# Sample tokens of a hybrid decoder layer: the threshold search spread over the projection blocks, the attention placed beside the first feed-forward half

## The chip, the core and the metric

The kernel runs on one core of a Trainium2 chip. The metric is the device time of one execution in microseconds. Before the change it is 2087.43 us, the median of 3 runs (2083.59 to 2090.55).

## What is computed

One layer for 1024 prompt tokens and 8 sample tokens (one new token each, with 4096 cached positions). One input projection feeds two head groups: sparse softmax attention, whose positions an indexer picks, and an RWKV-7 recurrence. Their outputs go through one output projection and a SwiGLU feed-forward. What matters here is the sample tokens' attention:

```python
def sample_attention(q, k_new, v_new, qi, ki_new, wi, cache_k, cache_v, cache_ik, page_table):
    ...
    score = indexer_scores(qi, ki_all, wi)           # 4096 cached positions and the new one
    ...
    _, idx = lax.top_k(score, n_sel)                 # 256 of them
    ...
    return attend_selected(q, pick(cache_k, k_new), pick(cache_v, v_new), valid)

def decoder_layer(x, c, attn_fn, prev_row, s0, lp):
    ...
    att = attn_fn(q, k, v, qi, ki, wi).reshape(B, T, ATT_W)
    rw, s_fin, last_row = rwkv7_mix(pr, prev_row, s0, lp)
    x = x + gate1 * (jnp.concatenate([att, rw], axis=-1) @ lp['w_out'])
    h2 = rms_norm(x, lp['norm2_g']) * (1 + scale2) + shift2
    ffn = (jax.nn.silu(h2 @ lp['w_ffn_gate']) * (h2 @ lp['w_ffn_up'])) @ lp['w_ffn_down']
    return x + gate2 * ffn, (k, v, ki, s_fin, last_row)
```

## The kernel before

Every large product is done as three matmuls on float32r halves (`mm_fm`, line 270 of the profile): each weight tile is loaded raw by SyncE's queue (SP, line 1625), rounded by ScalarE (`fh`, line 1629), and the rest is taken by VectorE or GpSimd (`fl`, line 1630). A projection block is 128 output columns: 8 contraction tiles x 3 products x 3 column groups = 72 matmuls.

In the program's order the stages are: modulation and norm; indexer scores of the prompt; then `qkv` with 12 projection blocks and `rw_project` with 14; the prompt's threshold search (`idx_select`, 26 halvings on VectorE and ScalarE); prompt attention in 4 head pairs of the first 512 queries (`att_pair`), 32 chunks of the modulation weights (`mod_chunk`, line 183; its row is copied by line 186 and transposed by line 189), the RWKV recurrence in 16 units (`rw_run`), attention of the second 512 queries; the output projection of the first half (`out_part`, line 1555); the feed-forward of the first half (`ffn`, gate and up in line 270, down in line 1666) in 10 pairs of 128 columns; the sample tokens' recurrent step (`smp_rwkv`) and `shift_out`; the output projection of the second half with the sample tokens; the last pair of the first half; the feed-forward of the second half.

This is the order of the trace only. The framework plans the instructions of each engine ahead of the run: on each engine an instruction that is ready in the plan goes first if it was traced first, and later work fills what is left. On the chip every engine and every DMA queue then runs its list strictly in order. `issue_after(ins)` is an edge without a wait: instructions traced in its block stand behind `ins` on the engine that they share.

The sample tokens' work up to their attention is a generator, `sample()`: `smp_scores` (16 groups of cached indexer keys, one `yield` each), `smp_select` and `smp_att`. `side(n)` pulls n steps. `SQ` gives the steps after each block of `qkv`, `SP_` those before each block of `rw_project`; all are 3, 78 in all, and 53 are wanted.

`smp_select` finds the 256th largest score per sample token. It opens with the largest and smallest score (a transpose, line 774, and a broadcast product, line 780), then runs 13 iterations: VectorE compares 256 scores per partition with 3 thresholds (line 796) and counts (line 797), TensorE sums the counts over the partitions with a matrix of ones (`allsum`, line 742), VectorE moves the lower bound. Each iteration ends in a `yield`, so its sum is traced in the same step as its count. After a last sum come the list of chosen rows (8 one-hot steps, line 869) and its way through DRAM into `kvrow`, the row numbers for the gathers; `seln` says whether the new token is chosen.

`smp_att` gathers for each of the 8 tokens 256 key rows (two indirect DMAs from GpSimd's queue, line 1285), loads the new key's row (line 1288) and the query spread over 128 partitions (line 1297) over SP, mixes the new row in (lines 1289, 1290), multiplies (line 1298) and sums (line 1299) on VectorE; then the softmax (lines 1303 to 1313); then the same gathers for the values and 4 matmul passes a token (line 1323), with lines 1331 and 1335 taking the heads apart. The query has one buffer, the large tiles four. The result goes to `d_mix[4]` (line 1339).

`smp_rwkv` uses a pool of its own, `smp3`, opened when the recurrence's pool `tR` is closed. It writes the other half of `d_mix[4]` (line 1471). The pools of the second half (`h2B`, `wfB`) are opened after `smp3` and the recurrence's constants are closed; `out_part` loads `d_mix` there (line 1524).

Of the kernel before, what the change touches and what calls it, by code (L numbers as in the profile page):

```python
# [7 lines left out]
F32 = mybir.dt.float32  # L8
F32R = mybir.dt.float32r
BF16 = mybir.dt.bfloat16  # L10
I32 = mybir.dt.int32
# [7 lines left out]
NS = 8  # L19
# [3 lines left out]
CW = 344  # L23
# [12 lines left out]
def bc(ap, shape):  # L36
    return ap.to_broadcast(list(shape))
# [29 lines left out]
WA = (2, 2, 2)  # L67
WB = (3, 3, 3)
SPL = 0
SQ = (3, 3, 3, 3, 3, 3, 3, 3, 3, 3, 3, 3)  # L70
SP_ = (3, 3, 3, 3, 3, 3, 3, 3, 3, 3, 3, 3, 3, 3)


class Ring:
# [10 lines left out]
class Kern:  # L85
# [253 lines left out]
    def rw_project(self, h, wp, tp, side):  # L339
        nc = self.nc  # L340
        for n_, j in enumerate([12, 13] + [o + p for p in range(4) for o in (4, 0, 8)]):
            side(SP_[n_])
            w = self.wload(self.I["w_in"][0], ATT_COLS + 128 * j, 128, wp)
            pr = tp.tile([128, NT + 1], F32, name="pr", bufs=2)
            X = tp.tile([128, T], F32, name="X", bufs=2)
            nc.gpsimd.memset(pr[:, 0:1], 0.0)
            for c in range(NC3):
                ps = self.ps.tile([128, 512], F32, name="ps")
                self.mm_fm(ps, CW, w, 0, 128, h, CW * c)
                nc.scalar.activation(pr[:, 1 + CW * c:1 + CW * c + CW], ps[:, :CW], AF.Copy)  # L350
                n = min(CW, T - CW * c)
                nc.scalar.activation(X[:, CW * c:CW * c + n], ps[:, :n], AF.Copy, scale=self.omm[:, j:j + 1])
            nc.vector.scalar_tensor_tensor(X, pr[:, 0:T], self.prm("rw_mu", j), X, op0=OP.mult, op1=OP.add)
            nc.gpsimd.tensor_copy(self.sh[:, j, :], pr[:, T:T + 9])
            nc.sync.dma_start(self.d_x[j], X)
# [383 lines left out]

    def allsum(self, x, n):  # L740
        ps = self.pS.tile([128, 512], F32, name="ps")
        self.nc.tensor.matmul(ps[:, :n], self.ones, x, start=True, stop=True)
        return ps[:, :n]

    def smp_prefix(self, x, rs, out, tp):
# [18 lines left out]
    def smp_select(self, tp, sp, dp):  # L764
        nc = self.nc
        v = sp.tile([128, 10, NS], F32, name="sbis")
        lo, hi, w, mid, cnt, t, new, tmp = (v[:, k, :] for k in range(8))
        s3 = self.ss.rearrange("p (b z) l -> p b (z l)", z=2)
        mm = tp.tile([128, 16], F32, name="mm", bufs=1)
        nc.vector.tensor_reduce(mm[:, 0:8], s3, axis=AX.X, op=OP.max)  # L770
        nc.vector.tensor_reduce(mm[:, 8:16], s3, axis=AX.X, op=OP.min)
        nc.vector.tensor_scalar(mm[:, 8:16], mm[:, 8:16], -1.0, None, op0=OP.mult)
        ps = self.pS.tile([128, 512], F32, name="ps")
        nc.tensor.transpose(ps[:16, :128], mm, self.ident)
        m1 = tp.tile([16, 1], F32, name="m1", bufs=1)
        nc.vector.tensor_reduce(m1, ps[:16, :128], axis=AX.X, op=OP.max)
        m2 = tp.tile([16, 16], F32, name="m2", bufs=1)
        nc.vector.tensor_scalar(m2, self.ident[:16, :16], m1, None, op0=OP.mult)
        ps = self.pS.tile([128, 512], F32, name="ps")
        nc.tensor.matmul(ps[:, :16], self.ones[:16, :], m2, start=True, stop=True)  # L780
        nc.vector.tensor_tensor(hi, ps[:, 0:8], self.snew, op=OP.max)
        nc.vector.scalar_tensor_tensor(lo, ps[:, 8:16], -1.0, self.snew, op0=OP.mult, op1=OP.min)
        self.bis_open(lo, hi, w, t)
# [7 lines left out]
        for k in range(self.NIT // 2):  # L791
            nc.vector.tensor_scalar(wk, w, 0.25 ** (k + 1), None, op0=OP.mult)
            nc.vector.tensor_tensor(md, fr, up(wk), op=OP.mult)
            nc.vector.tensor_tensor(md, md, up(lo), op=OP.add)
            cmp_ = tp.tile([128, 3, NS, 32], F32, name="sa_", bufs=self.SB["sa_"])
            nc.vector.tensor_tensor(cmp_, bc(s3[:, None], [128, 3, NS, 32]), bc(md[:, :, :, None], [128, 3, NS, 32]), op=OP.is_ge)
            nc.vector.tensor_reduce(cn, cmp_, axis=AX.X, op=OP.add)
            nc.vector.tensor_tensor(nw, up(self.snew), md, op=OP.is_ge)
            ps = self.allsum(cn.rearrange("p j b -> p (j b)"), 3 * NS)
            nc.vector.tensor_tensor(cn, ps.rearrange("p (j b) -> p j b", j=3), nw, op=OP.add)  # L800
            nc.vector.scalar_tensor_tensor(cn, cn, TOPK - 0.5, up(wk), op0=OP.is_ge, op1=OP.mult)
            nc.vector.tensor_reduce(t, cn.rearrange("p j b -> p b j"), axis=AX.X, op=OP.add)
            nc.vector.tensor_tensor(lo, lo, t, op=OP.add)
            yield
        self.bis_close(lo, hi, w, t)
        sel = tp.tile([128, 16, 16], F32, name="sc_", bufs=self.SB["sc_"])
        tie = tp.tile([128, 16, 16], F32, name="sc_", bufs=self.SB["sc_"])
# [8 lines left out]
        nc.vector.tensor_tensor(gtn, self.snew, hi, op=OP.is_gt)  # L816
        nc.vector.tensor_tensor(tin, self.snew, lo, op=OP.is_ge)
        nc.vector.tensor_tensor(tin, tin, gtn, op=OP.subtract)
        ps = self.allsum(cnt, NS)
        nc.vector.tensor_tensor(cnt, ps, gtn, op=OP.add)  # L820
        nc.vector.tensor_scalar(t, cnt, -1.0, TOPK + 0.5, op0=OP.mult, op1=OP.add)
# [6 lines left out]
        nc.vector.tensor_tensor(sel, sel, pf, op=OP.add)  # L828
        nc.vector.scalar_tensor_tensor(tmp, tot, 1.0, t, op0=OP.add, op1=OP.is_le)
        nc.vector.tensor_tensor(tmp, tmp, tin, op=OP.mult)  # L830
        self.seln = sp.tile([128, NS], F32, name="seln")
        nc.vector.tensor_tensor(self.seln, gtn, tmp, op=OP.add)

        self.smp_prefix(sel, rs, pf, tp)
# [21 lines left out]
        for z in range(2):  # L856
            c = slice(128 * z, 128 * z + 128)
            ps = self.pS.tile([128, 512], F32, name="ps")
            for k0 in range(0, 32, 8):
# [8 lines left out]
                for k in range(8):  # L868
                    nc.tensor.matmul(ps[0:64, 0:64], oh[:, k].rearrange("p b h -> p (b h)"), ov[:, k].rearrange("p b h -> p (b h)"),
                                     start=(k0 + k == 0), stop=(k0 + k == 31))  # L870
# [4 lines left out]
            nc.vector.tensor_reduce(l1, t4.rearrange("p b l -> p l b"), axis=AX.X, op=OP.add)  # L875
            nc.vector.tensor_copy(li[:, z, :], l1)
            nc.sync.dma_start(d[4 * z:4 * z + 4].rearrange("b (s l) -> (b s) l", l=16), li[:, z, :])
        self.kvrow = sp.tile([128, NS, 2], I32, name="kvrow")
        for z in range(2):
            nc.sync.dma_start(self.kvrow[:, :, z], d[:, 128 * z:128 * z + 128].rearrange("b s -> s b"))  # L880

# [22 lines left out]
    def qkv(self, h, wp, tp, cp2, side):  # L904
        nc, I = self.nc, self.I
# [9 lines left out]
        for j in range(12):  # L915
            n, p = "qkv"[j // 4], j % 4
            w = self.wload(I["w_in"][0], 128 * j, 128, wp)
            f = tp.tile([128, NT], F32, name="F", bufs=2)
            for c in range(NC3):
                ps = self.ps.tile([128, 512], F32, name="ps")  # L920
                self.mm_fm(ps, CW, w, 0, 128, h, CW * c)
                nc.scalar.activation(f[:, CW * c:CW * c + CW], ps[:, :CW], AF.Copy)
            y = tp.tile([128, 9, 128], F32, name="y", bufs=1)
            if n != "v":
# [1 line left out]
            for g in range(3):  # L926
                ps = self.ps.tile([128, 512], F32, name="ps")
# [18 lines left out]
            nc.sync.dma_start(outs[n][1][:, cs], y[:NS, 8, :])  # L946
            side(SQ[j])

# [777 lines left out]
    def build(self):  # L1726
        tc, nc, I, O = self.tc, self.nc, self.I, self.O
        with ExitStack() as ctx:
# [17 lines left out]
            if True:  # L1746
                with ExitStack() as c1:
# [3 lines left out]
                    with (tc.tile_pool(name="mA", bufs=2) as mp, tc.tile_pool(name="h1x", bufs=3) as xp,  # L1751
                          tc.tile_pool(name="h1f", bufs=1) as fp):
                        self.xt = []
                        c = self.craw = mp.tile([9, D], F32, name="c_raw", bufs=1)
# [11 lines left out]
                        h = self.norm_T(hp, mp, xp, fp)  # L1766
# [3 lines left out]
                    smp = cS.enter_context(tc.tile_pool(name="smp", bufs=1, side="right"))  # L1770
# [14 lines left out]
                    def sample():  # L1785
                        yield from self.smp_scores(smp, rp)
                        yield from self.smp_select(smp, rp, dp)
                        yield from self.smp_att(smp)

                    sgen = sample()  # L1790

                    with tc.issue_after(self.lastmm.ins):
# [39 lines left out]
            smp = cr.enter_context(tc.tile_pool(name="smp2", bufs=1, side="right"))  # L1832
# [32 lines left out]
            self.SB = {"sa_": 4, "sc_": 6}  # L1865
            self.pS = Ring(self.psr, self.psr, self.psr, self.psc)
            with tc.tile_pool(name="smp3", bufs=1) as smp:
                self.smp_rwkv(smp, dp)
                self.shift_out(smp)
            ce.close()  # L1870
# [51 lines left out]
```

## Time and profile before

| | us |
|---|---|
| median of 3 runs | 2087.43 |
| lowest, highest | 2083.59, 2090.55 |
| the profiled execution | 2080.43 |
| its span, first to last instruction | 2078.6 |
| TensorE busy | 1946.7 |
| VectorE busy | 1225.0 |
| ScalarE, GpSimd busy | 796.7, 793.4 |

The span is about 2 us shorter than the execution. [...] Overlapping matmuls count as busy once, and a busy TensorE at half clock does half the work. A wait is put down to the engine whose signal came last.

### The profile page before, as it was taken

To read this page: it belongs to the slowest core of one execution; us is meant where nothing else is said; L and a number is where in the kernel's file an instruction comes from. 1 tells how busy PE (TensorE), PEld (TensorE's weight loads), DVE (VectorE), ACT (ScalarE), POOL (GpSimd) and SP (SyncE) were. 2 spreads that over 40 slices of the span, in tenths; PEclk is the share of its full clock that TensorE was granted. 3 is DMA by queue.
4 is the path that set the end of the run, shared out by engine and by line. 5 is a ranking of instruction groups with operands and counts; after the bars stand their busy time and mean duration, and the time that the engine had idled before them with its cause. 6 is when DMAs were issued, how large, how long until landed. Compare 5 with 4: busy or idle time off the path is not lost.

```text
span 2078.6 us, 38421 instructions
## 1 busy us (share of the span) xinstructions
PE 1946.7 (94%) x14794; PEld 1677.5 (81%) x14794; DVE 1225.0 (59%) x2980; ACT 796.7 (38%) x1590; POOL 793.4 (38%) x1381
## 2 busy tenths in 40 slices
PE   5999999889996998999997979999999999999998
PEld 3878898879993567777766957777888999999998
DVE  6777988997547565667666354557544453121225
ACT  5466667523322343555544332222322332222221
POOL 2411255443454064667555420100411344545452
PEclk8999999989996787999998989999999999999999
DMA  8311233333238574232215322333633324323233
GB/s 262 87 31 31 63 112 97 92 86 107 72 123 261 146 187 114 62 78 76 54 37 157 92 81 84 123 118 113 177 101 104 102 92 142 91 93 92 92 93 113
DMA packets 303204, 220.25 MB, mean 106 GB/s; under 512 B 67151, under 2 KB 281650, under 8 KB 303022
## 3 DMA queue, kind: packets, MB, share of 16 engines
q1 hardware_dynamic: 298140, 200.99, 32.9%
q0 software_dynamic: 4864, 16.78, 2.6%
q8 instruction: 116, 1.90, 0.4%
q14 instruction: 66, 0.54, 0.1%
q10 hardware_dynamic: 18, 0.04, 0.0%
HBM read 187.11 MB, written 30.13 MB: 105 GB/s over the span
## 4 chain that ended last, share of the span: by engine, by line
PE 61%; DMA 7%; DVE 3%; POOL 2%; issue 1%; SPq 1%; ACT 1%; DVEq 0%; ACTq 0%; POOLq 0%
PE ps L270 27%; PE ps L1666 11%; PE ps L1555 3%; PE ps L1264 2%; PE ps L1253 2%; PE ps L1233 1%; PE ps L972 1%; DMA qt<-out_dram 1%; DMA d_t<-arr 1%; PE ps L183 1%; PE ps L388 1%; POOL itmp L1021 1%; PE ps L1052 1%; PE ps L1234 1%; PE ps L1059 1%
## 5 line engine op out<-in xcount | busy, mean ns | idle before, releaser
L1629 ACT ACTIVATE fh<-fr 128x1024 fp32r<-128x1024 f32 (+1 forms) x183 | 190.8, 1055 | 508.6 <-PE ps L270 278.6
L1630 POOL TENSOR_TENSOR fl<-fr,fh 128x1024 fp32r<-128x1024 f32 (+1 forms) x109 | 264.6, 2433 | 312.7 <-ACT fh L1629 310.5
L270 PE MATMUL ps<-h2hi,fh 128*128 128x264 f32 (+2 forms) x1056 | 337.2, 321 | 2.3 <-ACT fh L1629 1.9
L270 PE MATMUL ps<-h2lo,fh 128*128 128x264 f32 (+2 forms) x1056 | 335.8, 319 | 1.0 <-DVE h2lo L1604 1.0
L270 PE MATMUL ps<-h2hi,fl 128*128 128x264 f32 (+2 forms) x1056 | 333.4, 320 | 3.2 <-DVE fl L1630 3.0
L270 PE MATMUL ps<-h1hi,fh 128*128 128x344 f32 (+1 forms) x752 | 250.7, 333 | 1.9 <-ACT rl L556 1.3
L270 PE MATMUL ps<-h1lo,fh 128*128 128x344 f32 (+1 forms) x752 | 247.6, 329 | 0.0
L270 PE MATMUL ps<-h1hi,fl 128*128 128x344 f32 (+1 forms) x752 | 246.9, 328 | 0.0
L270 PEld LDWEIGHTS ps<-h2hi,fh 128*128 128x128 f32 x1056 | 199.0, 189 | 19.2 <-ACT fh L1629 6.0
L270 PEld LDWEIGHTS ps<-h2hi,fl 128*128 128x128 f32 x1056 | 197.7, 188 | 20.4 <-DVE fl L1630 6.9
L270 PEld LDWEIGHTS ps<-h2lo,fh 128*128 128x128 f32 x1056 | 199.0, 188 | 14.6 <-DVE h2lo L1604 1.4
L1021 POOL TENSOR_TENSOR itmp<-la,arr 128x24 f32<-128x24 f32 (+23 forms) x496 | 131.5, 265 | 181.9 <-DMA la<-d_l 146.0
L1655 DVE TENSOR_TENSOR fa<-fa,ps 128x256 f32<-128x256 f32 (+1 forms) x66 | 33.8, 512 | 255.1 <-PE ps L270 255.0
L1666 PE MATMUL ps<-al,fh 128*128 128x512 f32 (+2 forms) x528 | 165.6, 319 | 0.2 <-DVE al L1657 0.2
L1677 DVE TENSOR_TENSOR acc<-acc,ps 128x512 f32<-128x512 f32 (+2 forms) x224 | 107.7, 514 | 88.8 <-PE ps L1666 88.5
L1666 PE MATMUL ps<-ah,fl 128*128 128x512 f32 (+2 forms) x528 | 159.8, 319 | 0.0
L1666 PE MATMUL ps<-ah,fh 128*128 128x512 f32 (+2 forms) x528 | 156.9, 321 | 0.0
L270 PEld LDWEIGHTS ps<-h1hi,fh 128*128 128x128 f32 x752 | 144.2, 192 | 8.2 <-ACT rl L556 3.4
L1023 POOL TENSOR_TENSOR arr<-arr,itmp 128x24 f32<-128x24 f32 (+23 forms) x496 | 135.5, 273 | 38.3
L270 PEld LDWEIGHTS ps<-h1hi,fl 128*128 128x128 f32 x752 | 144.0, 192 | 2.5 <-issue 2.5
L270 PEld LDWEIGHTS ps<-h1lo,fh 128*128 128x128 f32 x752 | 144.1, 192 | 2.4 <-issue 2.1
L1630 DVE TENSOR_TENSOR fl<-fr,fh 128x1024 fp32r<-128x1024 f32 x74 | 96.1, 1304 | 84.4 <-ACT fh L1629 82.9
(939 smaller groups left out, 4208.3 us busy)
## 6 DMA issues: line engine op xcount, KB each, us to landing
fr<-in_w_ffn_gate_dram SPq DMA_DIRECT2D x44, 512.0 KB
fr<-in_w_ffn_up_dram SPq DMA_DIRECT2D x44, 512.0 KB
fr<-in_w_ffn_down_dram SPq DMA_DIRECT2D x44, 512.0 KB
fr<-in_w_in_dram SPq DMA_DIRECT2D x34, 512.0 KB
wr<-in_w_ada_dram SPq DMA_DIRECT2D x8, 1024.0 KB
la<-d_l SPq DMA_DIRECT2D x16, 512.0 KB
fr<-in_w_out_dram SPq DMA_DIRECT2D x16, 512.0 KB
d_x<-X SPq DMA_DIRECT2D x14, 512.0 KB
```

Of the source, the lines that this page charges most:

```text
L183: nc.tensor.matmul(ps[32 * g:32 * g + 32, :cw], self.cT[:, k, :], w[:, k, :], start=(k < 4), stop=(k >= 4))
L270: mm = nc.tensor.matmul(ps[:m, :n], a[:, k, wc:wc + m], b[:, k, t0:t0 + n], start=(k == 0 and i == 0), stop=(k == kd - 1 and i == 2))
L1021: ie.tensor_tensor(t3, bc(la[:, s, s + 1:][:, None, :], [128, nu, nt]), bc(arr[:, 0:nu, s:s + 1], [128, nu, nt]), op=OP.mult)
L1023: ie.tensor_tensor(arr[:, 0:nu, s + 1:], arr[:, 0:nu, s + 1:], t3, op=OP.subtract)
L1253: nc.tensor.transpose(ps[:, 128 * (l % 4):128 * (l % 4) + 128], P[e][:, 128 * l:128 * l + 128], ident)
L1264: nc.tensor.matmul(po[o, 0:128], vt[:, l, o], PT[e][:, 128 * (l % 4):128 * (l % 4) + 128], start=(l == 0), stop=(l == i))
L1555: nc.tensor.matmul(p3[:, t, :], a[:, k, ts], b[:, k % 4, :], start=(k == 0 and n == 0), stop=(k == KD - 1 and n == 2))
L1629: nc.scalar.activation(hi, raw, AF.Copy)
L1630: self.loe.tensor_tensor(lo, raw, hi.bitcast(F32), op=OP.subtract)
L1655: nc.vector.tensor_tensor(a, a, pu[:, :n], op=OP.mult)
L1666: nc.tensor.matmul(ps[:, :n], a[:, 0, 128 * o:128 * o + 128], b[:, c:c + n], start=(i == 0), stop=(i == 5))
L1677: nc.vector.tensor_tensor(a, a, ps[:, :n], op=OP.add)
```

## The change

`SQ` becomes 3 for the first six blocks of `qkv` and 1 for the last six, `SP_` is 1 throughout: 38 steps in all. `smp_select` yields just ahead of each sum instead of after the iteration, so the count is traced in one step and its sum in the next; it also yields ahead of the transpose, the broadcast product and the sum of the ties, which gives it 24 steps. These products and all sums are issued behind `self.lastmm`, which `qkv` and `rw_project` now set to the last matmul of each column group. `smp_att` leaves the generator: it is run whole in the pool `smp3`, just ahead of `smp_rwkv`. `seln` and `kvrow` move to the pool of constants, so that they live that long.

```diff
-SQ = (3, 3, 3, 3, 3, 3, 3, 3, 3, 3, 3, 3)
-SP_ = (3, 3, 3, 3, 3, 3, 3, 3, 3, 3, 3, 3, 3, 3)
+SQ = (3, 3, 3, 3, 3, 3, 1, 1, 1, 1, 1, 1)
+SP_ = (1, 1, 1, 1, 1, 1, 1, 1, 1, 1, 1, 1, 1, 1)
@@ rw_project, and in the same way qkv
-                self.mm_fm(ps, CW, w, 0, 128, h, CW * c)
+                self.lastmm = self.mm_fm(ps, CW, w, 0, 128, h, CW * c)
@@ allsum
-        self.nc.tensor.matmul(ps[:, :n], self.ones, x, start=True, stop=True)
+        with self.tc.issue_after(self.lastmm.ins):
+            self.nc.tensor.matmul(ps[:, :n], self.ones, x, start=True, stop=True)
@@ smp_select
+        yield
         ps = self.pS.tile([128, 512], F32, name="ps")
-        nc.tensor.transpose(ps[:16, :128], mm, self.ident)
+        with self.tc.issue_after(self.lastmm.ins):
+            nc.tensor.transpose(ps[:16, :128], mm, self.ident)
...
+        yield
         ps = self.pS.tile([128, 512], F32, name="ps")
-        nc.tensor.matmul(ps[:, :16], self.ones[:16, :], m2, start=True, stop=True)
+        with self.tc.issue_after(self.lastmm.ins):
+            nc.tensor.matmul(ps[:, :16], self.ones[:16, :], m2, start=True, stop=True)
...
             nc.vector.tensor_tensor(nw, up(self.snew), md, op=OP.is_ge)
+
+            yield
             ps = self.allsum(cn.rearrange("p j b -> p (j b)"), 3 * NS)
...
             nc.vector.tensor_tensor(lo, lo, t, op=OP.add)
-            yield
...
+        yield
         ps = self.allsum(cnt, NS)
...
-        self.seln = sp.tile([128, NS], F32, name="seln")
+        self.seln = self.cp.tile([128, NS], F32, name="seln")
...
-        self.kvrow = sp.tile([128, NS, 2], I32, name="kvrow")
+        self.kvrow = self.cp.tile([128, NS, 2], I32, name="kvrow")
@@ build
                         yield from self.smp_select(smp, rp, dp)
-                        yield from self.smp_att(smp)
...
             with tc.tile_pool(name="smp3", bufs=1) as smp:
+                for _ in self.smp_att(smp):
+                    pass
                 self.smp_rwkv(smp, dp)
```

## Rows read from the trace of the kernel before

**Rows 1.** The page, part 1: busy time, share of the span, instructions.
```profile
PE 1946.7 (94%) x14794; PEld 1677.5 (81%) x14794; DVE 1225.0 (59%) x2980; ACT 796.7 (38%) x1590; POOL 793.4 (38%) x1381
```

**Rows 2.** Busy time by stretch: length, engines in turn, granted clock, DMA share, GB/s.
```profile
380.00:470.00 90.00, 74.22 (x445) 71.80 (x444) 84.92 (x158) 27.44 (x54) 36.88 (x26) 0.89 0.33 92
470.00:620.00 150.00, 149.35 (x1027) 145.00 (x1026) 88.48 (x182) 45.65 (x100) 60.15 (x52) 1.00 0.33 99
620.00:700.00 80.00, 61.80 (x492) 33.61 (x491) 59.59 (x175) 20.59 (x53) 26.93 (x32) 0.79 0.73 217
700.00:850.00 150.00, 138.66 (x1309) 100.06 (x1311) 83.50 (x344) 61.96 (x162) 71.50 (x263) 0.80 0.55 139
850.00:1100.00 250.00, 242.88 (x2780) 186.51 (x2778) 174.91 (x672) 128.32 (x301) 154.82 (x575) 0.99 0.24 62
1306.00:1460.00 154.00, 149.47 (x676) 119.09 (x675) 92.96 (x154) 37.19 (x47) 11.36 (x5) 0.99 0.38 115
```

**Rows 3.** Waits, 380 to 470 us: waiter, line <- releaser: us in total, times, longest.
```profile
PE ps L742 <- DVE q L797: 9.9, 3, 5.2
PE ps L774 <- DVE bis L603: 5.3, 1, 5.3
```

**Rows 4.** The chain that ended last, in a projection block: start, us, what.
```profile
516.91 6.38 PE ps L270 x40
```

**Rows 5.** Waits, 590 to 700 us.
```profile
ACT P L1244 <- DVE mx L1243: 22.7, 6, 10.9
...
PE ps L189 <- DVE mrow L186: 10.6, 4, 8.7
...
PE ps L1217 <- POOL kn L1212: 3.3, 1, 3.3
```

**Rows 6.** VectorE in order of time, 604 to 647 us: start, us, instruction, idle before.
```profile
605.22 1.23 DVE L1298 TENSOR_TENSOR sa__4367<-sa__4367,sq__4374 128x1024 f32<-128x1024 f32 x1 [0.45 <-DMA sa__4367<-in_cache_k_dram,kvrow]
...
626.47 1.23 DVE L1298 TENSOR_TENSOR sa__4504<-sa__4504,sq__4511 128x1024 f32<-128x1024 f32 x1 [1.70 <-DMA sq__4511<-d_qs]
...
631.15 0.27 DVE L186 COPY mrow<-ps 128x128 f32<-128x128 f32 x1
...
646.42 1.23 DVE L1298 TENSOR_TENSOR sa__4630<-sa__4630,sq__4637 128x1024 f32<-128x1024 f32 x1 [1.07 <-DMA sq__4637<-d_qs]
```

**Rows 7.** Line 1285, the gathers: duration ns min/median/max, first and last start.
```profile
L1285 POOL DMA_INDIRECT sa__4493<-in_cache_k_dram,kvrow x2: 1172/1553/1934, 600.1 to 605.3; - x2
...
L1285 POOL DMA_INDIRECT sa__4902<-in_cache_v_dram,kvrow x2: 942/944/947, 665.8 to 667.0; - x2
```

**Rows 8.** Groups of VectorE, 590 to 700 us: busy us, mean ns, idle before.
```profile
L1299 DVE TENSOR_REDUCE sc__4366<-sa__4367 128x16 f32<-128x1024 f32 x1 | 1.2, 1200 | 0.0
...
L1290 DVE SCALAR_TENSOR_TENSOR sa__4367<-kvn,seln,sa__4367 1x512 f32<-1x512 f32 x1 | 0.7, 740 | 0.0
```

**Rows 9.** The chain that ended last, 655 to 695 us, one token's value products.
```profile
675.81 1.81 PE ps L1323 x4
```

**Rows 10.** Instructions in order of time on GpSimd and SP, around the sample step.
```profile
1306.69 0.11 POOL L1361 MEMSET xa<- 128x16 f32 x1 [98.76 <-DMA d_mix<-y]
...
1459.60 1.77 SPq L1471 DMA_DIRECT2D d_mix<-sc__17335  x4
1462.52 0.92 SPq L1524 DMA_DIRECT2D fr<-d_mix  x2
```

**Rows 11.** The chain that ended last, from 1310 us on.
```profile
1315.43 10.27 PE ps L270 x44
...
1353.41 10.28 PE ps L270 x44
...
1487.45 1.67 PE ps L1555 x14
...
1640.95 8.28 PE ps L1555 x70
...
1688.56 19.76 PE ps L270 x165
```

More of the change, by code (lines that the diff above doesn't have):

```diff
@@ L920, in qkv @@
                 ps = self.ps.tile([128, 512], F32, name="ps")
-                self.mm_fm(ps, CW, w, 0, 128, h, CW * c)
+                self.lastmm = self.mm_fm(ps, CW, w, 0, 128, h, CW * c)
                 nc.scalar.activation(f[:, CW * c:CW * c + CW], ps[:, :CW], AF.Copy)
```

## Prediction

> **What bounds the kernel now.** I read the page first. TensorE is busy 94% of the span [rows 1], so a gain can only come where it is idle or runs at a low granted clock. The next view is busy time by stretch [rows 2]. For each stretch I take what TensorE loses as length minus (busy time x granted clock), an estimate that counts a half-clock microsecond as half. From 470 to 620 us the loss is 150 - 149.35 x 1.00 = 0.7 us. Two stretches that the change touches lose much: 380 to 470 loses 90 - 74.22 x 0.89 = 23.9 us, and 620 to 700 loses 80 - 61.80 x 0.79 = 31.2 us. 700 to 850 loses 39, and 850 to 1100 only 9.5 in 250.
>
> The waits say why. From 380 to 470 TensorE waits 9.9 us at the sample search's sum (line 742) for the count of line 797 and 5.3 us at line 774 for VectorE [rows 3]: 15.2 of the 15.8 us that it is idle there. VectorE itself is busy 84.92 of 90 us [rows 2], since the prompt's own search shares it; so the sum stands in TensorE's order before its operand is there. From 590 to 700 the costliest wait of TensorE is 8.7 us at line 189, for the copy of line 186; that copy stood on VectorE behind sample attention's product of line 1298, which itself waited 1.70 us for its query load [rows 5, 6]. The softmax of the prompt's attention (line 1244) lost up to 10.9 us at once in the same way, and line 1217 lost 3.3 us to GpSimd, whose queue carries the sample's 32 gathers [rows 5, 7]. So in one stretch the search, in the other the sample attention, sits in in-order queues ahead of work that TensorE needs.
>
> **The change part by part.**
>
> *The search.* Nothing is added but order. Sixteen small matmuls (the transpose, the 16-row broadcast, 13 sums of the iterations, one of the ties) get an edge that puts them behind the last matmul of the projection block traced before, and the generator yields just ahead of each, so that the operand is made during one block and summed at its end. A block of 72 matmuls lasts 72 x 6.38 / 40 = 11.5 us [rows 4], in which VectorE has one iteration of the sample's search to do where it now has three, so the operand is normally there. What is queued behind a late sum is the whole next block, as before. With both waits and the clock back, 380 to 470 would lose 0.4 us (the rate of 470 to 620), so the upper end is 23. Lower end: VectorE stays nearly full until the prompt's search ends, a few of the sixteen steps still fall there, and only the clock or one wait returns: 5. I take 16, near the named 15.2, since most steps move behind the full part. The list then ends late: of 38 calls, 16 go to the scores and 22 to the selection's 24 steps, so two of its eight one-hot groups come after the prompt's search in the trace. Nobody needs the list before the new attention, so I cost it at nothing; its DMAs stood in SP's queue near the same place before. If that cover failed, a wait like that of line 1217, 3.3 us [rows 5], would be added.
>
> *Sample attention leaves 620 to 700.* It takes from there 32 gathers on GpSimd, 16 row loads and 8 broadcast query loads on SP, over 8 x (1.23 + 1.20) + 16 x 0.74 = 31 us of VectorE [rows 6, 8], and on TensorE 8 x 1.81 = 14.5 us at full clock [rows 9], say 15 with its transposes. The stretch's progress is 61.80 x 0.79 = 48.8 us of full-clock work, so 34 remain. At the rate of the stretch behind it, 700 to 850, 138.66 x 0.80 / 150 = 0.74 [rows 2], these take 46 us: a gain of 34. Lower end: the head pairs of prompt attention are a serial chain, and only the two named waits go, 8.7 + 3.3 = 12. Upper end: no loss at all, 46. I take 30, nearest to the neighbouring stretch, which holds the same pairs, modulation chunks and recurrence units without sample attention. From 850 to 1100 TensorE is nearly full [rows 2], so what is gained ahead of it is kept; late next are the pairs' loads.
>
> *Sample attention arrives beside the first half's feed-forward.* TensorE gets its 15 us back in full, because it has little to hide them there: 1306 to 1460, where the sample's recurrent step already runs, loses 154 - 149.47 x 0.99 = 6.0 us [rows 2]. Every instruction comes along. On SP its 24 loads stand among weight loads that wait for one of two raw buffers, on VectorE its products stand ahead of weight splits (line 1630), and TensorE waits for these. This mixture isn't in the trace. Nearest is that same stretch, whose 6.0 us I scale up, as this step's VectorE work is larger: 10. The lower end is 3, half of it; the upper end is the 31 us that 620 to 700 lost beside the same work.
>
> *Who waits for it.* The new pool of the sample step opens when the last recurrence unit has been written, as GpSimd's wait until 1306.69 shows, and the sample's mix was written at 1459.60 to 1461.4 [rows 10]. Only after the pool closes does the second half's output projection load its mix, 1462.52; its matmuls begin at 1487.45, its last long run ends at 1649.2, and the second half's feed-forward starts at 1688.56 [rows 10, 11]. That run did 70 matmuls in 8.28 us, so a chunk of 96 + 16 takes 13 us and four take 53. At its fastest the chain is 25 + 53 + 39 = 117 us. With 15 us more on TensorE the feed-forward would start at 1704, so the pool may close up to 1704 - 117 - 1461 = 126 us later without cost. How much later? Attention's eight key products are (646.42 - 605.22) / 7 = 5.9 us apart [rows 6], so 47 us; its value part has three turns on TensorE, which low priority lets in once per feed-forward pair, 1353.41 - 1315.43 = 38 us [rows 11]: at most 114 us, and at least some 34, the eight value products of 1.81 us and as much again for waits. So 81 to 161, in the middle 121: I cost this at nothing, with 0 and 161 - 126 = 35 as its ends.
>
> Sum: -16 - 30 + 15 + 10 + 0 = -21 us. The profiled execution took 2080.43 us (span 2078.6 and 1.8 around it), so 2059.4; the median of the runs shown lies 7.0 us higher at 2087.43, and the prediction for a median is 2087.4 - 21 = 2066. All good ends give -23 - 46 + 15 + 3 = -51, all bad ones -5 - 12 + 15 + 31 + 35 = +64.
>
> [...] Of 32 gathers on GpSimd the short ones took 0.94 us and the longest 1.93 [rows 7], with VectorE at work beside them. [...] By the row's longest, all 32 gathers are worth 32 us on the chain above, which makes its 121 us 153 and the output projection 27 us late: 2093 in place of 2066, and that belongs to the first rival.
>
> **The rivals.**
> 1. *Slower: the second half is starved.* The attention and then the recurrent step, which share four large buffers, hold the pool so long that the output projection comes too late for the feed-forward pair that should cover it. For it: the middle of the chain is only 5 us under the slack. Against: SP, GpSimd and DMA are lightly loaded there. It decides from 126 us; from 147 us it has eaten the gain, and from 153 it shows as a loss. At 161 plus half the gathers' 32, 177 us, the price is 51: 2066 + 51 = 2117.
> 2. *No change: the pairs bind.* Prompt attention's head pairs stay as far apart as now whatever else runs, the stretch gains only the 15 us of moved work, the search 10, and the feed-forward gives 15 + 10 back: 2087.
> 3. *The search doesn't do what it says.* VectorE is late at every block's end instead of at four places: 16 waits of 1 us take the place of 15.2, and the sum is -30 + 15 + 10 + 1 = -4: 2083.
> 4. *More:* search 20, stretch 40, feed-forward 15 + 5: -40, 2047.
>
> **How the numbers follow.** Forecast 0.55, rival 1 0.15, rival 2 0.12, rival 3 0.08, rival 4 0.10. About 0.3% (6 us) is what a measurement here can tell from no change. Faster: 0.55 + 0.10 + half of rival 3 = 0.69; same: 0.12 + 0.04 = 0.16; slower 0.15. The range reaches from below rival 4 to above rival 2, with a part of rival 1: 2042 to 2100.
>
> **What would show it.** Right: no wait of several microseconds at lines 742 and 774; from the last projection on, no wait at line 189 near 9 us, and a stretch of 80 us after it with less than 20 lost; GpSimd's gathers in the middle of the first half's feed-forward, with TensorE's idle time there under 15 us; the second half's feed-forward 15 to 35 us earlier than 1688. Wrong: long waits at line 270 for line 1630 while the gathers run, idle time at lines 1555 or 1597 ahead of the second half, or prompt attention as far from the last projection as before.

## The result, and the profile after

The changed kernel takes 2101.7 us (median), the kernel before 2088.8 us beside it: a ratio of 1.0073, 95% interval 1.0053 to 1.0093. It is 13 us slower; 2066 was predicted, with 2100 as the upper end. A second series gave 1.0049 (1.0019 to 1.0078).

The profiled execution took 2117.7 us, at the slow end of the kernel's own runs (2093 to 2118), and that of before 2080.4, near the fast end of its own (2074 to 2106). Their difference of 37 us is therefore not the change's price; prices below come from ratios of many runs, and the profiles say where and why. (A ratio is made into microseconds with 2090: 0.1% is 2 us.)

Busy time by stretch in the changed kernel, columns as in [rows 2]:
```profile
380.00:470.00 90.00, 74.42 (x441) 71.99 (x440) 84.30 (x156) 27.62 (x55) 37.05 (x26) 0.89 0.31 90
470.00:620.00 150.00, 149.46 (x1026) 144.77 (x1025) 79.17 (x170) 45.63 (x98) 42.70 (x46) 1.00 0.23 75
620.00:700.00 80.00, 67.16 (x579) 44.12 (x570) 43.41 (x186) 28.65 (x74) 19.96 (x65) 0.71 0.64 170
700.00:850.00 150.00, 127.61 (x1260) 93.31 (x1257) 72.38 (x290) 56.20 (x143) 64.30 (x246) 0.76 0.50 126
850.00:1100.00 250.00, 244.76 (x2681) 186.89 (x2679) 169.17 (x655) 123.80 (x290) 146.40 (x549) 0.96 0.24 59
1306.00:1460.00 154.00, 141.06 (x599) 105.00 (x600) 96.81 (x149) 36.61 (x46) 34.81 (x27) 0.96 0.45 135
1600.00:1725.00 125.00, 125.00 (x779) 111.96 (x778) 66.34 (x88) 42.34 (x78) 43.14 (x25) 1.00 0.32 104
```
The granted clock is given as a share of full speed. The trace of the kernel before shows what a share of 0.50 does: the 128x344 matmuls of a projection start 0.287 us apart at 0.50 (396.83 to 399.41 us) and 0.157 us apart at 1.00 (434.12 to 436.94 us), so TensorE does 0.55 of the work there; the losses count it as half, as in the prediction.

The first row is that of before almost to the digit: 74.42 busy at 0.89, where [rows 2] has 74.22 at 0.89. The search's edit changed nothing there. The waits of TensorE from 380 to 470 us (us in total, times, longest) say the same, against 9.9 and 5.3 in [rows 3]:
```profile
PE ps L744 <- DVE q L803: 9.6, 3, 5.2
PE ps L778 <- DVE bis L604: 5.3, 1, 5.3
```
The feed-forward row lost 6.0 us before and now 154 - 141.06 x 0.96 = 18.6 (9.9 in a second profile of the same kernel, after_again below). The stretch of the head pairs, 620 to 850, loses 32.3 + 53.0 = 85.3 us here (70.8 in after_again), where [rows 2] has 31.2 + 39.1 = 70.3: the loss that was to go from there is still there. The last row shows no starved second half: TensorE is busy in all 125 us.

In TensorE's program order the reason for the first row is plain. Of each of the search's sixteen matmuls (the transpose, the broadcast, 13 sums, the sum of the ties) this is the number of the projections' matmuls (line 270, in the changed kernel 271) that stand ahead of it; a block has 72:
```
before   1104 1125 1176 1213 1248 1293 1345 1405 1452 1488 1536 1582 1622 1667 1704 1744
changed  1104 1125 1176 1213 1248 1293 1345 1405 1452 1488 1536 1582 1622 1680 1752 1824
later5   1248 1320 1392 1464 1536 1608 1680 1752 1824 1869 1908 1955 1992 2034 2068 2108
```
The trace of the kernel before has the sixteen start behind just these numbers of matmuls, and the 767 transfers that SyncE issues and ScalarE's 1429 instructions start in it in the program's order. The first thirteen stand at the same instruction in both kernels. Fewer calls per block and the anchors changed the trace order, but not the place. (later5 is an experiment below.)

What the edit did move is the end of the search. The second half of the list of chosen rows leaves SyncE's queue 35 us later, among the loads of the head pairs; in the kernel before, then in the changed one:
```profile
591.49 0.46 SPq L877 DMA_DIRECT2D d_list<-listi  x1
```
```profile
626.63 0.47 SPq L885 DMA_DIRECT2D d_list<-listi  x1
```
TensorE now waits for the list (620 to 680 us), and the fourth of the eight head-pair steps writes its result no earlier than before, though the sample attention has left the stretch:
```profile
PE ps L877 <- POOL sa__6164 L875: 2.6, 1, 2.6
```
```profile
787.13 0.87 SPq L1272 DMA_DIRECT2D d_mix<-OT  x2
```
```profile
798.01 0.99 SPq L1280 DMA_DIRECT2D d_mix<-OT  x2
```
(The second row is of the kernel before, the third of the changed one; in after_again it is 787.4.)

### The profile page after: what moved, and what is told of

The parts are those of the page before. It is cut to its first block, busy times and chain, and to the rows that moved or that the text cites. A ratio compares the mean times of both kernels' runs of the same rounds, so it can differ in the third digit from the quotient of the medians.

```text
span 2115.6 us, 38431 instructions
## 1 busy us (share of the span) xinstructions
PE 1969.7 (93%) x14794; PEld 1693.0 (80%) x14794; DVE 1226.0 (58%) x2980; ACT 801.1 (38%) x1592; POOL 784.0 (37%) x1381
## 3 DMA queue, kind: packets, MB, share of 16 engines
q1 hardware_dynamic: 298140, 200.99, 32.3%
## 4 chain that ended last, share of the span: by engine, by line
PE 61%; DMA 6%; DVE 4%; issue 3%; POOL 2%; ACT 1%; SPq 0%; DVEq 0%; POOLq 0%; ACTq 0%
PE ps L271 26%; PE ps L1674 10%; PE ps L1563 4%; PE ps L1272 3%; PE ps L1261 2%; PE ps L1241 1%; PE ps L980 1%; PE ps L184 1%; PE ps L389 1%; PE ps L1242 1%; PE ps L1067 1%; DVE fl L1638 1%; DMA qt<-out_dram 1%; PE ps L1073 1%; PE ps L1060 1%
```

## The experiments

Each ratio is to the kernel before in the same series, with its 95% interval.

**One half of the change at a time.** search_only takes the attention's move back:
```diff
@@ build (against the changed kernel)
                         yield from self.smp_select(smp, rp, dp)
+                        yield from self.smp_att(smp)
...
-                for _ in self.smp_att(smp):
-                    pass
```


> The changed kernel with the sample attention put back into the generator, so that only the search's edit is left. Theory A (the planner had already put one sum of the search into each projection block, so the edit changes next to nothing; the loss comes from the moved attention): within 5 us of the kernel before, about 2089 us, and TensorE again waits 9 to 10 us at the search's sums. Rival B (the edit makes the list late, and the late list costs at the head pairs): 2097 to 2102 us, like the whole change. The prediction's own step: 16 us faster, 2073 us.

Measured: 2116.1 us, 1.0111 (1.0073 to 1.0149). It is slower than the whole change, and than any of the three expectations. The sums' waits are 9.7 and 5.3 us again. The generator reaches the attention later, and it lies deeper in the head pairs: its 32 gathers start from 634.1 to 717.5 us, in the kernel before from 595.7 to 672.5. Two of them (ns min/median/max, first and last start):
```profile
L1293 POOL DMA_INDIRECT sa__6188<-in_cache_k_dram,kvrow x2: 942/1018/1093, 634.1 to 639.3; - x2
...
L1293 POOL DMA_INDIRECT sa__6369<-in_cache_v_dram,kvrow x2: 946/1055/1164, 716.2 to 717.5; - x2
```
So the run doesn't give the price of the search's edit alone: the list and the attention come later together.

att_only is the kernel before with smp_att taken out of the generator, traced ahead of smp_rwkv as in the changed kernel, and seln and kvrow in the constant pool.

> The kernel before with only the sample attention moved beside the first half's feed-forward; the search as it was. Theory A: like the whole change, 2098 to 2106 us. Rival B: near the kernel before, 2087 to 2092 us. The prediction's own terms for this part (-30 + 15 + 10): 5 us faster, 2084 us.

Measured: 2097.5 us, 1.0034 (1.0009 to 1.0058): 7 us slower. The move loses by itself, without the search's edit. Of the 13 us by which the changed kernel is slower, that leaves 6 to the search's edit, with an uncertainty about as large.

**Without the attention.** old_none and new_none are the kernel before and the changed kernel with the attention replaced (in old_none its line goes from the generator, and the new line stands ahead of smp_rwkv):
```diff
-                for _ in self.smp_att(smp):
-                    pass
+                self.smp_zero(smp)      # writes the same d_mix rows from a zero tile
```


> The kernel before without the sample attention: its rows of the mix are written as zeros instead. This part of the computation is left out, and the time is read as what the sample attention costs where it stood. Prediction: 30 us less than before (2059 us). Rival (the head pairs bind, only TensorE's own 15 us come back): 2074 us. If the stretch behind gives back what is gained: 2080 us or more.

> The changed kernel without the sample attention (rows of the mix written as zeros; this part is left out): changed kernel minus this is what the sample attention costs beside the first half's feed-forward. Theory A: that cost is about 30 us (15 of matmuls and as much in waits), so 2072 us, and the same as the kernel before without it within 4 us. Rival B: 10 us or more above the kernel before without it, since the search's edit is in both. The prediction: 25 us less than changed, 2077 us.

Measured: 2068.4 us, 0.9893 (0.9860 to 0.9925), and 2066.3 us, 0.9875 (0.9841 to 0.9910). So the attention costs 1.07%, 22 us, where it stood. Where it went it costs 0.34 + 1.07 = 1.41%, 29 us, with the old search, and 39 us with the new one (0.61%, the mean of the changed kernel's two series, + 1.25). The uncertainty of these three prices is 7 to 9 us each. The two kernels without the attention agree within the intervals: by them the search's edit is worth 4 us less time, and nothing that can be told from zero.

Whether the late list costs (Rival B of the expectations) is not settled by that. With the attention out of the stretch and the old hand-out, the fourth pair writes its result at 759.4 us (att_only) and 766.8 (old_none), and TensorE doesn't wait for the list. In all eight profiles of kernels that have the edit's hand-out and no attention there (the changed kernel twice, new_none, rwkv_first and the four late_ kernels) it writes it at 787 to 798, and TensorE waits 2.3 to 2.9 us for the list and 6.1 to 6.8 for the queries of the next pair. From 620 to 850 us the two lose 54 and 60, the eight 71 to 85. The ratios give the edit much less: 6 us from att_only to the changed kernel, -4 from old_none to new_none, with 6 and 10 us of uncertainty. Which part of the edit's hand-out holds the pairs back is not isolated: no run has the edit's places with the early list, and later5, below, has a list that is later still and early pairs.

**Moving the sums for good.** later5 hands the steps out so that, by program order, the transpose stands two projection blocks later and the next sums one block apart:
```diff
-SQ = (3, 3, 3, 3, 3, 3, 1, 1, 1, 1, 1, 1)
-SP_ = (1, 1, 1, 1, 1, 1, 1, 1, 1, 1, 1, 1, 1, 1)
+SQ = (3, 3, 3, 3, 3, 1, 0, 0, 0, 0, 0, 1)
+SP_ = (1, 1, 1, 1, 1, 1, 1, 1, 2, 2, 2, 2, 2, 2)
```


> The changed kernel with the sample search's steps handed out later and with gaps, so that in TensorE's order the transpose stands two projection blocks later and the sums one whole block apart, behind the time in which VectorE is full; everything else as in the changed kernel (2102 us). If the prediction's mechanism was right and the edit only failed to move the sums, the waits of 9.7 and 5.3 us at the sums and the transpose go, and the time is 12 to 18 us lower, 2084 to 2090 us. Rival (VectorE's lateness comes out at other places, or the later list costs at the head pairs what the waits give): 2098 to 2108 us.

Measured: 2084.3 us, 0.9950 (0.9920 to 0.9980): 23 us under the changed kernel by the ratios (17 by the medians of the two series), and faster than the kernel before. One wait at a sum is left, 6.6 us. The same edit on new_none:

> The changed kernel without the sample attention (rows of the mix as zeros; this part is left out), with the search's steps handed out later as in the run that gained 17 us. Without the attention nothing else is moved, so this is the price of the search's place alone, against 2066 us for the same kernel with the edit's own places. If the sums' waits are that price: 2049 to 2056 us. Rival (that run gained because the head pairs fell differently around the attention, not at the sums): 2061 to 2071 us.

Measured: 2046.5 us, 0.9774 (0.9735 to 0.9812), against 0.9875: 1.01%, 21 us give or take 11, with no attention that could fall differently. Its waits from 380 to 470 us, and its busy time there and behind:
```profile
PE ps L744 <- DVE q L803: 5.3, 1, 5.3
PE ps L939 <- ACT F L930: 4.4, 3, 3.0
```
```profile
380.00:470.00 90.00, 80.25 (x499) 77.80 (x499) 71.12 (x118) 32.13 (x65) 41.08 (x30) 0.94 0.38 107
470.00:620.00 150.00, 145.87 (x1019) 139.01 (x1017) 92.07 (x228) 47.08 (x101) 34.22 (x43) 0.99 0.27 89
```
The transpose's wait is gone, two of three waits at the sums too, and the stretch loses 14.6 in place of 23.8; 470 to 620 then loses 5.6 in place of 0.5. The best mark is the last copy of the projections, last start in the row of ScalarE's copy X; this row of the changed kernel, then of later5_none:
```profile
L353 ACT ACTIVATE X<-ps,omm x42: 533/542/549, 440.5 to 618.4; 128x344 f32<-128x344 f32 x28, 128x336 f32<-128x336 f32 x14
```
```profile
L353 ACT ACTIVATE X<-ps,omm x42: 532/541/547, 428.1 to 604.6; 128x344 f32<-128x344 f32 x28, 128x336 f32<-128x336 f32 x14
```
The projections end at 604.6 (604.5 in later5), 14 us earlier than in the changed kernel and 11 earlier than in new_none, which has the same rest (615.9). In the kernels with the old places, before and changed among them, that copy starts between 615 and 622. The other 10 of the 21 us lie behind it: by one profile of each the fourth pair writes its result at 756.2 us, in new_none at 790.7. So the rival of the expectation has a part in the gain, even without the attention.

later8 moves the transpose five blocks and the sums five to seven, by program order (SQ all 0 behind its first six entries, SP_ = 0, 0, 1, 1, 1, 1, then 2).

> The changed kernel with the search's steps later still: the transpose five blocks, the sums five to eight blocks behind the edit's places. If what counts is that VectorE is free by then: the last wait at a sum goes too and the projections end within 2 us of the run with two blocks (604.5 us), or up to 5 us earlier; the time is 2078 to 2088 us. If the late list costs at the head pairs: over 2090 us.

Measured: 2086.6 us, 0.9936 (0.9905 to 0.9968). The waits at the sums are gone, the last copy starts at 598.3, and the time is that of later5: the last 6 us were not kept behind the projections. Which waits went fits VectorE's load: in the kernel before it is busy 18 us or more in every 20 up to 460 us and 14 to 16 from there to 540, and its waits at the sums all lie ahead of 460. Of later5's sums only the first, the one that waits, stands there, of later8's none.

**What the attention costs beside the feed-forward.** Three kernels cut one resource each, the fourth all three:
```diff
@@ late_few_gathers
+            nc.gpsimd.memset(k, 0.0)
-            for z in range(2):
+            for z in range(2 if b == 0 else 0):
@@ late_small_dve: k[:, :, :32] in place of k in the products, sums and row replacements
@@ late_small_pe
-  nc.tensor.matmul(po[32 * i:32 * i + 8, :], pt[:, z, b, :], v[:, z, :], ...)
+  nc.tensor.matmul(po[32 * i:32 * i + 8, 0:64], pt[:, z, b, :], v[:, z, 0:64], ...)
```


> The changed kernel with 4 of the sample attention's 32 gathers; the other rows are set to zero on GpSimd, so this part of the computation is left out. If the gathers (GpSimd's queue and the transfers) make the 35 us that the attention costs beside the feed-forward, 2085 us or less; if VectorE's queue and TensorE's own work make it, 2098 to 2103 us.

> The changed kernel with the attention's products, sums and row replacements on VectorE cut to a sixteenth of their columns (left out for the rest), so that some 27 us of VectorE's work go and everything else stays. If VectorE's queue makes the waits of the feed-forward, 15 us less than the changed kernel: 2084 to 2090 us. If the gathers or TensorE's own work do, 2097 to 2103 us.

> The changed kernel with the attention's value products on TensorE cut from 512 to 64 columns (the other heads left out). The prediction's term of 15 us for TensorE's own work is tested: 2088 us if it is right, since seven eighths of it go. Rival (the products share TensorE, since they write different row groups and three of them start in the same microsecond of the trace): 4 us or less, 2098 to 2102 us.

> The changed kernel with all three cuts to the sample attention at once: 4 of 32 gathers, a sixteenth of VectorE's columns, an eighth of the value products' columns (left out for the rest). What stays is its chain of small steps and its loads. If the 35 us are the three resources, any one of which is enough for a part: 2066 to 2075 us. If they are the chain (the sample's recurrent step comes 100 us later and meets other work): 2088 to 2098 us.

Measured: 2091.0 us, 1.0009 (0.9976 to 1.0042); 2097.6 us, 1.0030 (0.9996 to 1.0064); 2108.8 us, 1.0100 (1.0064 to 1.0137); all three 2085.7 us, 0.9944 (0.9913 to 0.9975). The changed kernel stands at 1.0061 and new_none at 0.9875, so the gathers are worth some 11 us (3 to 19, and the zeros that GpSimd writes in their place are in it), VectorE's work 6 (no more than the uncertainty of 8), and all three together 24 of the 39. The third came out 8 us slower than the kernel that it was cut from, with 9 us of uncertainty: no gain from the narrow products can be told.

Another measure is the time from the first to the last down product of both feed-forwards, which leaves out the stretches ahead of it; all 32 late gathers lie inside it. First and last start, in the changed kernel, new_none and late_all_small:
```profile
L1674 PE MATMUL ps<-ah,fh x528: 274/284/794, 1264.6 to 2106.3; 128*128 128x512 f32 x59, 128*128 128x256 f32 x59, 128*128 128x264 f32 x58
```
```profile
L1680 PE MATMUL ps<-ah,fh x528: 274/284/628, 1256.4 to 2063.6; 128*128 128x512 f32 x59, 128*128 128x256 f32 x59, 128*128 128x264 f32 x58
```
```profile
L1675 PE MATMUL ps<-ah,fh x528: 274/284/582, 1261.0 to 2080.0; 128*128 128x512 f32 x59, 128*128 128x256 f32 x59, 128*128 128x264 f32 x58
```
That is 841.7 us with the attention (836.4 in after_again), 807.2 without (811.5 before), 826.2 with few gathers, 831.3 with small VectorE work, 835.1 with narrow value products, 819.0 with all three cut. With the other hand-outs of the search it is 846.7 (att_only) against 810.3 (old_none), and 850.3 (later5) against 812.1 (later5_none): the attention costs 36 and 38 us there, 29 to 34 with the edit's places. One execution each; the order of the cuts agrees with the ratios except for the value products, which save 1 to 7 us here. Some 12 us stay when all three are cut.

**Two other places for that cost.** rwkv_first traces smp_rwkv and shift_out ahead of smp_att; later5_rwkv_first is that with later5's hand-out; later5_rf_poolq is the same with the attention's loads of kvn and of the query issued by GpSimd.

> The changed kernel with the sample's recurrent step traced ahead of its attention, so that the recurrent step stands where it stood in the kernel before. If the displaced recurrent step makes a part of the 35 us: 2088 to 2096 us. If the attention costs the same wherever it stands beside the feed-forward: 2098 to 2106 us. The prediction's first rival (the second half is starved, since the last of the two chains ends near its slack): the feed-forward of the second half starts late and the time stays over 2100 us.

> The search's steps handed out later (the run that gained 17 us, 2084 us) and the sample's recurrent step traced ahead of its attention (the run that gained 6 us against its neighbour). If the two are independent: 2075 to 2081 us, below both kernels. If the second was scatter: 2082 to 2088 us.

> The kernel of the run beside this one, with the attention's 24 small and broadcast loads issued from GpSimd's queue in place of SyncE's. If they held weight loads up in SyncE's queue: 5 to 10 us less than the run beside it. If it is the transfers themselves (the gathers and the broadcasts on the same DMA engines): no change within 4 us.

Measured: 2095.9 us, 1.0014 (0.9986 to 1.0042), beside the changed kernel's 1.0049 in the same series; 2084.3 us, 0.9939 (0.9908 to 0.9969); 2087.5 us, 0.9956 (0.9929 to 0.9984). Against later5's 0.9950 the order of the two steps is worth nothing that can be told, so the 6 us of the first were scatter or don't add up, and moving the loads to the other queue gives back nothing that can be told. The three kernels with the sums really moved and the attention late, and later8, are all 0.4 to 0.6% faster than the kernel before; among themselves the runs don't tell them apart.

The changed kernel once more:

> The changed kernel once more, for a second profile and for times on the chip of its neighbours here. 2097 to 2106 us; TensorE again waits 5.3 us at the transpose and 9 to 10 us at the sums.

Measured: 2102.1 us, 1.0049 (1.0019 to 1.0078), with waits of 10.2 us at the sums and 5.3 at the transpose.

## Why the prediction was wrong, point by point

**The search, -16 us predicted, -4 to +6 measured (failed).** The step "VectorE has one iteration of the sample's search to do where it now has three" took the generator's calls for the place of the work. The calls set only the order in which it is traced; the planner had spread the sums already. A row of the trace of before would have said so: the 13 sums (26 passes) start from 410.6 to 516.6 us, 8.8 us apart, in blocks of 11.5 us [rows 4].
```profile
L742 PE MATMUL ps<-q,c_one x26: 183/269/407, 410.6 to 516.6; 128*128 128x24 f32 x26
```
An edge to the block traced before is no change where the sum stood behind it anyway; that this is how the planner came to the same place is argued from the positions, not shown. The lower bound of 5 fell too, since it took for granted that at least one wait would go; neither did. The price of the stretch was of the right size: moved for good, the sums give 21 us (later5_none, 10 to 32), against 16. Only part of that is the waits: the projections end 11 to 14 us earlier, and the rest lies behind them. Rival 3 came nearest, but it put VectorE's lateness at the new places; the places were the old ones. The -4 is new_none to old_none, the +6 the changed kernel to att_only, and the two differ by no more than their uncertainty.

A second step failed with it. The prediction cost the late list at nothing, because "its DMAs stood in SP's queue near the same place before". They did not: its last part stood at 591.5 us and is now at 626.6. For that case it names a wait of 3.3 us; 2.6 were measured, in TensorE's wait for the list. And its own sign of being wrong came, "prompt attention as far from the last projection as before": from the last projection copy to the fourth pair's result it was 167 us, and is 180 (169 in after_again), where att_only has 142. That the late list does this, and what it costs in the end, is not shown.

**The attention leaves 620 to 700, -30 predicted, -22 measured** (the interval of old_none gives 16 to 29; right in kind, inside its bounds, too large). Sample attention's waits are gone: from 620 to 850 us line 189's 10.6 are 0.7 in old_none, line 1217's 7.1 are 2.1. The next late thing is what the prediction named in half a sentence, "the pairs' loads": the changed kernel's longest waits of TensorE from 620 to 850 us are for transfers, where [rows 5] has VectorE and GpSimd.
```profile
PE ps L184 <- DMA sa__7292<-in_w_ada_dram: 6.8, 1, 6.8
PE ps L1211 <- DMA qt<-d_q: 6.7, 1, 6.7
```
In after_again they are 2.6 and 6.5. The second, at 809 us, belongs to the edit's hand-out (old_none and att_only don't have it); their longest wait for a transfer is 4.5 and 4.3, a load of the modulation weights.

From 620 to 850, old_none loses 59.8 us where before lost 70.3 (80 - 72.31 x 0.77 and 150 - 137.97 x 0.83, against [rows 2]): 10 us less loss, and the attention's own matmuls on top. The rate that the prediction took held: (72.31 x 0.77 + 137.97 x 0.83) / 230 = 0.74. Two smaller things fell short of it: the attention's matmuls are worth 11 to 13 us and not 15 (next point), and 850 to 1100, where what is gained was to be kept, loses 14.4 us in old_none and 9.5 before. These are single profiles, and the changed kernel's two differ by 15 us in this stretch, so how the 8 us divide is not shown. In the changed kernel none of the gain can be seen there, as said above.

**Beside the first half's feed-forward, +25 predicted, +29 to +39 measured** (mis-sized). Of the two terms, TensorE's own 15 us was somewhat too high: all 52 matmuls of the attention keep it busy 12.5 us in the changed kernel (the 32 value products 9.6, where 14.5 was taken) and 11.4 in att_only. In the trace value products of different samples, which write different 32-row groups of one tile, overlap: four start within 0.03 us, where those of one sample start 0.43 us apart. In order of time on TensorE (start, us, tiles):
```profile
1393.82 0.60 PE L1331 MATMUL ps<-sa__17190,sc__17186 128*8 128x512 f32 x1
1393.83 0.60 PE L1331 MATMUL ps<-sa__17199,sc__17186 128*8 128x512 f32 x1
1393.84 0.60 PE L1331 MATMUL ps<-sa__17208,sc__17186 128*8 128x512 f32 x1
1393.85 0.60 PE L1331 MATMUL ps<-sa__17217,sc__17186 128*8 128x512 f32 x1
```
Fourteen such matmuls, nearly four samples, end within 1.9 us, where I had 1.81 us for each sample [rows 9]; of the other four samples two run alone and two overlap in part. The stalls are the term that was too small. What 29 to 39 us leave for them is 17 to 27, where 10 was predicted. The trace shows a part: TensorE's waits from 1232 to 1725 us add up to 20.5 us (18.1 in after_again, 21.5 in att_only), in before to 5.1, in new_none to 7.1, so 11 to 16 us are waits. The largest in the changed kernel:
```profile
PE ps L1674 <- ACT fh L1637: 5.3, 2, 5.1
PE ps L271 <- DVE fl L1638: 4.3, 5, 1.3
PE ps L1674 <- DVE al L1665: 3.9, 2, 3.7
```
The first is a weight load. SyncE issued it among loads of the residual and a broadcast, while GpSimd issued ten gathers from 1292.8 to 1308.0; it reached ScalarE's copy 15.2 us later, which TensorE then waited for:
```profile
1294.49 0.51 SPq L1633 DMA_DIRECT2D fr<-in_w_ffn_down_dram  x1
```
```profile
1309.70 1.06 ACT L1637 ACTIVATE fh<-fr 128x1024 fp32r<-128x1024 f32 x1 [4.35 <-DMA fr<-in_w_ffn_down_dram]
```
In the kernel before ScalarE waits for a down weight once in this feed-forward, 0.5 us. That the gathers held the load up is not shown: late_few_gathers, with 4 of them, has such a wait of ScalarE of 7.4 us, and att_only and later5, with all 32, have no wait of TensorE over 0.3 us for such a copy, while the attention costs them no less. The second is what the prediction described, products ahead of weight splits in VectorE's queue:
```profile
1320.57 1.20 DVE L1307 TENSOR_REDUCE sc__17084<-sa__17096 128x16 f32<-128x1024 f32 x1
...
1322.30 0.73 DVE L1298 SCALAR_TENSOR_TENSOR sa__17107<-kvn,seln,sa__17107 1x512 f32<-1x512 f32 x1
1322.96 0.67 DVE L1685 TENSOR_TENSOR acc<-acc,ps 128x512 f32<-128x512 f32 x1
1323.55 2.34 DVE L1638 TENSOR_TENSOR fl<-fr,fh 128x1024 fp32r<-128x1024 f32 x2
```
The prediction moved the gathers along but gave their 8.4 MB no price; cut to 4 of 32, they are worth some 11 us by the ratio. What the 12 to 15 us are that stay with all three cut is open; neither another order of the two steps nor another queue for the loads gave anything back that can be told.

**The second half late, 0 predicted, 0 measured.** The sample's mix is written 99 us later, at 1560.6 (78 later in after_again), inside the 126 us that the prediction found free. TensorE does not stall at the second half's output projection, so the slower time is not rival 1, whose sign it has. (One end of that estimate doesn't add up: eight value products of 1.81 us and as much again are 29 us, not 34; it changes nothing.) For the gathers the prediction put 32 us on that chain by the longest of [rows 7]. Here the 32 gathers take 39 us in all, the longest 3.06, and in the kernel before 36, the longest 1.93; 32 times the short ones' 0.94 would be 30. What made them longer here is not shown by a run.

**The sum** by measured terms, with the search's edit as the step from att_only to the changed kernel: +6 - 22 + 29 = +13 us, the result. It closes because each term is a difference of two of the same runs, so it confirms nothing by itself. Of the miss of 34 us, 22 are then the search, 8 the stretch of the pairs, 4 the feed-forward; with the attention's cost taken in the changed kernel it is -4 - 22 + 39, and 12, 8 and 14. The search failed in either case, and the uncertainty doesn't choose between the two. Both gains lay in stretches whose loss I took as freed by the edit; for the search no row of the prediction said whether the edit moves anything in the engine's order.

## What to carry to other kernels

Where a planner sets the order, an edit of the trace order is a change only if the instruction's place in its engine's order moves: read the spacing of the starts in the trace of before against the length of the block they are to be tied to. Here the waits that VectorE's full stretch caused went when the waiting instructions were moved past that stretch. What follows at the end of a list that is spread out moves too, its transfers with it: look at what they will stand among. And work that is moved brings its transfers along: set its megabytes against the loads of the new neighbour.

## What had not been expected of the hardware

Two executions of the changed kernel, the same program, differ by 20 us between the last projection (618.4 and 618.3) and the first down product of the feed-forward (1264.6 and 1244.7), and by 5 us in the rest (841.7 and 836.4). The stretches of the head pairs, where TensorE stops and starts, were granted different clocks; of after_again:
```profile
620.00:700.00 80.00, 68.57 (x641) 46.21 (x637) 45.66 (x193) 29.93 (x77) 25.33 (x90) 0.79 0.70 185
700.00:850.00 150.00, 128.04 (x1287) 93.67 (x1288) 76.91 (x305) 59.08 (x153) 65.08 (x242) 0.82 0.48 119
```
0.79 and 0.82 stand against 0.71 and 0.76 in the first profile. Over the 20 runs of the changed kernel the time goes with the mean clock, from 2093 us at 0.961 to 2118 at 0.944; whether the clock or the stops come first is not shown. A single pair of profiles can't price a change of 10 us in such a stretch; a mark at its beginning and one at its end can say where it lies.
